# Two layers of a hybrid diffusion backbone on one core: the last two token tiles of the attention output projection, staggered by two weight rows

## The chip, the cores and the metric

The kernel is one program on one core of a Trainium2 chip. The metric is device time in microseconds (us) of one execution. The core has five engines, each with its own queue of instructions that it works off in order: TensorE (PE in the profile; PEld is its weight load), VectorE (DVE), ScalarE (ACT), GpSimd (POOL), and SyncE (SP), which here only issues DMAs. Engines wait for each other through semaphores. Matmul results land in PSUM, in banks of 128 x 512 floats; everything else lies in SBUF.

## The reference

Two layers over 1024 latent tokens (8 tiles of 128) and 256 context tokens. Layer 0 mixes tokens by a chunked gMLP, layer 1 by windowed attention; each is followed by a convolutional GLU. The change lies where layer 1's attention ends and its GLU begins:

```
y = moveaxis(out, 0, 1).reshape(bsz, n_tok, N_HEADS * HEAD_DIM) @ w_o      # output projection
x = x + g1 * rms_norm(y, norm_g[i, 1])
h = modulate(rms_norm(x, norm_g[i, 2]), sh2, sc2)
# conv_ffn(h):
a, b = split(h @ w_up, 2)              # 2 x 2816 columns
a = conv3(a) + conv_b                  # along the tokens
x = x + g2 * rms_norm((gelu(a) * b) @ w_down, norm_g[i, 3])
```

All of it is float32. The kernel multiplies by splitting each operand into a high part (`fp32r`) and a rest, so that one product is three matmuls: high x high, high x rest, rest x high.

## The kernel before, in words

`last_o` is the output projection of the last two token tiles, 6 and 7. The weight `w_o` comes in eight rows of 128 x 1024 (row k = 0 to 7): a DMA into `raw` (3 buffers), a cast on ScalarE into `wh`, and a subtraction on VectorE into `wl` (4 buffers each, shared with all other weights). Then twelve matmuls of 512 columns: for tile 6 and then tile 7, for both halves of 512 output columns, three each. The accumulators are two PSUM tiles `psA` of two banks; each holds one half of the columns for *both* token tiles, tile 6 in the first bank and tile 7 in the second.

After the eighth row each tile goes through `late_norm`, a generator with one step per `yield`: (1) load the residual row, sums of squares of both halves on ScalarE, products with the gate on VectorE; (2) the power on GpSimd, the residual sum on VectorE; (3) a second sum of squares on ScalarE, a power and the scaling of the row on GpSimd; (4) the flip: eight transposes on TensorE into a `psA` tile, scaled out of it by ScalarE and VectorE in turn, and a DMA of the flipped tile to `xT` in memory. `post_norm` is the like chain for tiles 4 and 5, which are in work when `last_o` starts (`tick` moves them on).

`lat_ffn` is the GLU. It needs its operands in eight combinations (`cmb`) of the flipped tiles: `combine(0)` builds them for tokens 0 to 511, `combine(1)` for 512 to 1023, in 16 steps each, from `xT`. `last_o` and the flips are the generator `between`: each of the 16 steps of `combine(0)` moves `between` one step. Then come the jobs. The first five column blocks of `w_up` are `up_plain` jobs, which need only the first half of the tokens: an X half of 48 matmuls of about 256 columns into two `psB` banks, and a Y half of 48 into a `psA` tile; weights again by cast and subtraction. After each quarter of a job, `step(fill)` moves the rest of `between` and then `combine(1)` one step. The jobs that follow need both halves of the operands.

The scheduler of the tile framework then lays out each engine's queue by its own estimates; in it, the X halves of jobs 1 and 2 come right after `last_o`, and the flips of tiles 6 and 7 stand inside job 2's X half.

Of the kernel before, what the change touches and what calls it, by code (L numbers as in the profile page):

```python
# [15 lines left out]
P = 128  # L16
D = 1024
KD = D // P
# [14 lines left out]
def hybrid_kernel(  # L33
# [23 lines left out]
    V, S, G, T = Engine(nc.vector, "V"), Engine(nc.scalar, "S"), Engine(nc.gpsimd, "G"), Engine(nc.tensor, "T")  # L57
    Q = Engine(nc.sync, "Q")
# [17 lines left out]
    def nm(s):  # L76
        uid[0] += 1
        return f"{s}_{uid[0]}"

    def t_raw():  # L80
        return sb.tile([P, 1024], F32, name=nm("raw"), tag="raw", bufs=3)

    def t_row(dt=F32, shape=(P, 1024)):
        return sb.tile(list(shape), dt, name=nm("row"), tag="row", bufs=10)
# [19 lines left out]
    def t_sm(w=2):  # L104
        return sb.tile([P, w], F32, name=nm("sm"), tag="sm", bufs=24)

    def t_w(tag, dt=F32R, shape=(P, 1024)):
        return sb.tile(list(shape), dt, name=nm(tag), tag=tag, bufs=4)
# [21 lines left out]
    def mm3(p, wh, wl, xh, xl, first, last):  # L130
        T.matmul(p, wh, xh, start=first, stop=False)
        T.matmul(p, wh, xl, start=False, stop=False)
        T.matmul(p, wl, xh, start=False, stop=last)
# [111 lines left out]
    gates = {}  # L245
# [5 lines left out]
    def step(gen, n=1):  # L251
        for _ in range(n):
            next(gen, None)
# [10 lines left out]
    def src_row(stage, t):  # L264
        if stage == 0:
            return x_in[0, t * P:(t + 1) * P, :] if t < 8 else ctx_in[0, (t - 8) * P:(t - 7) * P, :]
        return xs[stage][t * P:(t + 1) * P, :]
# [16 lines left out]
    def normed(src, dst, spare=None):  # L284
        r = rstd_of(src, spare)
        G.tensor_scalar(out=dst, in0=src, scalar1=r, scalar2=0.0, op0=ALU.mult, op1=ALU.add)
# [79 lines left out]
    active, mode = [], {"wide": False}  # L366

    def tick():
        for gen in list(active):
            if next(gen, 1):  # L370
                active.remove(gen)
# [8 lines left out]
    def gated(p, gate, y, part, junk):  # L380
        ss = t_sm(1)
        S.activation(junk, p, AF.Square, accum_out=ss)
        V.tensor_tensor(out=y, in0=p, in1=gate, op=ALU.mult)
        G.tensor_scalar(out=ss, in0=ss, scalar1=1.0 / D, scalar2=part, op0=ALU.mult, op1=ALU.add)
        return ss

    def late_norm(stage, t, banks, gate, mod, on_flip):
        xr = t_row()
        Q.dma_start(xr, src_row(stage, t))
        y = t_row()  # L390
        ss = EPS
        for h in range(2):
            hs = slice(h * 512, (h + 1) * 512)
            ss = gated(banks[h], gate[:, hs], y[:, hs], ss, y.bitcast(mybir.dt.bfloat16)[:, 1024 * h:1024 * h + 512])
        yield 0
        r = t_sm(1)
        G.tensor_tensor(out=r, in0=ss, in1=mhalf, op=ALU.pow)
        V.scalar_tensor_tensor(out=xr, in0=y, scalar=r, in1=xr, op0=ALU.mult, op1=ALU.add)
        yield 0
        normed(xr, y, y)  # L400
        S.dma_start(xs[stage + 1][t * P:(t + 1) * P, :], xr)
        yield 0
        xt = flip(stage + 1, t, y, mode["wide"], mod)
        on_flip(t, xt)

# [570 lines left out]
    def lat_ffn(l, stage, n0, halos, gate, between, steady, ctx=None, after=None):  # L976
# [120 lines left out]
        def up_plain(f, nxt, fill):  # L1097
            W, more = next_weights(nxt)
            X, X2, pY = psB(), psB(), psA()
            Y, Y2 = pY[:, 0, :], pY[:, 1, :]  # L1100
            for pair_, half in ((("b11", "b21"), X), (("b12", "b22"), Y)):
                for q in range(2):
                    for k in range(4):
                        wh, wl = (W[pair_[q]][z][:, k, :] for z in range(2))
                        c, kk = k // 2, k % 2
                        first = HL["a11" if q == 0 else "a12", c]
                        second = [A21[c][:, z] for z in range(2)] if q == 0 else [t[:, :, 0:256] for t in HL["a22", c]]
                        lead = 2 if half is X else 0
                        for out, src, lo, n in ((half[:, 0:256 + lead], first, 2 - lead, 256 + lead),
                                                ((X2 if half is X else Y2)[:, 0:256], second, 0, 256)):  # L1110
                            st, sp = q == 0 and k == 0, q == 1 and k == 3
                            xh, xl = (t[:, kk, lo:lo + n] for t in src)
                            T.matmul(out, wh, xh, start=st, stop=False, skip_group_check=True)
                            T.matmul(out, wh, xl, start=False, stop=False, skip_group_check=True)
                            T.matmul(out, wl, xh, start=False, stop=sp, skip_group_check=True)
                    step(fill)
                    step(more)
                if half is X:
                    a = t_row(shape=(P, 1028))
                    G.memset(a[:, 0:1], 0.0)  # L1120
                    S.copy(a[:, 1:257], X[:, 2:258])
                    S.copy(a[:, 513:514], X[:, 1:2])
                    S.copy(a[:, 257:513], X2[:, 0:256])
                    G.tensor_copy(keep[:, f:f + 1], a[:, 512:513])
            step(more, 9)
            conv_gate(f, a, 512, pY[:, :, 0:256], 0)
# [70 lines left out]
        if ctx is not None:  # L1197
            fill = chain(between, combine(0), combine(1))
        else:
# [6 lines left out]
            fill = chain(between, combine(1))  # L1206
        for (f, how), nxt in zip(jobs, jobs[1:] + [None]):
# [3 lines left out]
            if fill is not None:  # L1211
                step(fill, 100)
                fill = None
# [30 lines left out]
        for h in range(2):  # L1244
            pair = [psA() for _ in range(2)]
            banks = [pair[i // 2][:, i % 2, :] for i in range(4)] + [psB() for _ in range(4)]
            ws = {}
# [30 lines left out]
            for i in range(8):  # L1278
# [14 lines left out]
                for q in range(2):  # L1293
                    hs = slice(q * 512, (q + 1) * 512)
# [391 lines left out]
    orow, last_rows = {}, {}  # L1686
# [89 lines left out]
    for i in range(n_pairs + LC):  # L1776
# [13 lines left out]
        if i in (21, 24, 27):  # L1790
            t = 5 + (i - 21) // 3
# [16 lines left out]
    def last_o():  # L1808
        tiles = sorted(last_rows)
        acc = [psA() for _ in range(2)]  # L1810
        for k in range(KD):
            raw = t_raw()
            Q.dma_start(raw, w_o[0, k * P:(k + 1) * P, :])
            hi, lo = t_w("wh"), t_w("wl")
            S.copy(hi, raw)
            V.tensor_sub(lo, raw, hi)
            for i, t in enumerate(tiles):
                oh, ol_ = last_rows[t]
                for h in range(2):
                    hs = slice(h * 512, (h + 1) * 512)  # L1820
                    mm3(acc[h][:, i, :], oh[:, k, :], ol_[:, k, :], hi[:, hs], lo[:, hs], k == 0, k == KD - 1)
            tick()
            yield
        for i, t in enumerate(tiles):
            active.append(late_norm(2, t, [acc[h][:, i, :] for h in range(2)], gates[(1, 2, 0)], (1, 3), on4))
            yield

    tick()
# [44 lines left out]
```

## Time and profile before

| | |
|---|---|
| runs of before, median (lowest to highest of 3) | 2944.5 us (2943.89 to 2946.25) |
| the profiled execution | 2941.13 us |
| its span, first to last instruction | 2939.4 us |
| mean granted TensorE clock | 0.991 |
| TensorE busy | 2830.1 us, 96% of the span |
| VectorE / ScalarE / GpSimd busy | 69% / 46% / 23% |
| idle time of TensorE from 2190 to 2275 us, longest wait | 9.6 us, for GpSimd (`row`) |

The span leaves out 1.73 us before the first and after the last instruction. A row of the timeline gives the start, the duration and what an instruction writes and reads; a bracket at its end gives the idle time of that engine just before and what ended it. Durations of matmuls in a row overlap, so the pace is read from starts, or from the busy time of a window and its count. PEclk is the share of full TensorE clock that was granted: 1.00 is the level of 2.4 GHz, 0.50 that of 1.2 GHz.

### The profile page before, as it was taken

To read this page: it belongs to the slowest core of one execution; us is meant where nothing else is said; L and a number is where in the kernel's file an instruction comes from. 1 tells how busy PE (TensorE), PEld (TensorE's weight loads), DVE (VectorE), ACT (ScalarE), POOL (GpSimd) and SP (SyncE) were. 2 spreads that over 40 slices of the span, in tenths; PEclk is the share of its full clock that TensorE was granted. 3 is DMA by queue.
4 is the path that set the end of the run, shared out by engine and by line. 5 is a ranking of instruction groups with operands and counts; after the bars stand their busy time and mean duration, and the time that the engine had idled before them with its cause. 6 is when DMAs were issued, how large, how long until landed. Compare 5 with 4: busy or idle time off the path is not lost. (4 is left out here: it accounts for less than half of the span.)

```text
span 2939.4 us, 40162 instructions
## 1 busy us (share of the span) xinstructions
PE 2830.1 (96%) x14834; PEld 2406.6 (82%) x14834; DVE 2033.0 (69%) x3066; ACT 1353.9 (46%) x2279; POOL 683.9 (23%) x1003
## 2 busy tenths in 40 slices
PE   7999999999999999999999999899998999999999
PEld 5798988899898888888777777888887888888887
DVE  6557674756787878778643769887877777776333
ACT  4332342322575444543323534877775444444221
POOL 1151130720201212220003025564551212220000
PEclk9999999999999999999999999999999999999999
DMA  7764356532675333546845865356666333325532
GB/s 260 239 190 143 111 183 211 163 98 75 195 232 164 108 115 101 172 144 233 292 133 186 274 227 170 107 192 215 195 230 195 108 112 104 97 83 189 181 114 100
DMA packets 402310, 488.08 MB, mean 166 GB/s; under 512 B 17473, under 2 KB 296897, under 8 KB 402113
## 3 DMA queue, kind: packets, MB, share of 16 engines
q1 hardware_dynamic: 345697, 422.32, 44.8%
q10 hardware_dynamic: 55264, 58.99, 5.9%
q0 software_dynamic: 1152, 4.19, 0.4%
q8 instruction: 117, 1.92, 0.3%
q14 instruction: 80, 0.66, 0.1%
HBM read 388.96 MB, written 96.47 MB: 165 GB/s over the span
## 5 line engine op out<-in xcount | busy, mean ns | idle before, releaser
L50 PE MATMUL psB<-cmb,wh 128*128 128x512 f32 (+2 forms) x2584 | 757.3, 377 | 5.7 <-ACT row L50 2.6
L50 ACT CAST wh<-raw 128x1024 fp32r<-128x1024 f32 (+1 forms) x388 | 346.2, 904 | 490.8 <-PE psB L50 207.0
L50 PEld LDWEIGHTS psB<-cmb,wh 128*128 128x128 f32 x2584 | 472.2, 189 | 104.0 <-ACT row L50 4.9
L50 PE MATMUL psB<-cmb,wl 128*128 128x512 f32 (+2 forms) x1292 | 487.4, 377 | 0.0
L50 DVE TENSOR_TENSOR wl<-raw,wh 128x1024 fp32r<-128x1024 f32 (+1 forms) x388 | 400.0, 1043 | 124.2 <-ACT wh L50 119.7
L50 PE MATMUL psB<-wh,big 128*128 128x512 f32 x864 | 288.3, 401 | 1.4 <-ACT big L50 1.3
L50 PEld LDWEIGHTS psB<-cmb,wl 128*128 128x128 f32 x1292 | 243.6, 189 | 48.2
L50 POOL TENSOR_SCALAR sm<-sm 128x1 f32<-128x1 f32 (+1 forms) x76 | 41.3, 544 | 870.6 <-ACT tmp L50 320.6
L50 POOL TENSOR_TENSOR row<-raw,raw 128x512 f32<-128x512 f32 x44 | 76.4, 1736 | 602.1 <-DMA raw<-in_f_w_up_dram 485.9
L50 DVE TENSOR_TENSOR al<-raw,ah 128x1024 fp32r<-128x1024 f32 x74 | 90.5, 1224 | 170.9 <-ACT ah L50 170.5
L50 PE MATMUL psB<-wh,act 128*128 128x512 f32 x640 | 202.9, 395 | 1.6 <-DVE tmp L50 1.6
L50 PEld LDWEIGHTS psB<-wh,big 128*128 128x128 f32 x864 | 163.4, 190 | 41.1 <-ACT big L50 2.4
L50 PE MATMUL psA<-big,wh 128*128 128x320 f32 x1024 | 193.3, 311 | 3.0 <-ACT wh L50 1.8
L50 DVE SCALAR_TENSOR_TENSOR row<-row,cwcols,row 128x1024 f32<-128x1024 f32 (+2 forms) x142 | 160.9, 1133 | 38.4 <-issue 17.8
L50 ACT CAST ah<-raw 128x1024 fp32r<-128x1024 f32 x74 | 77.4, 1048 | 226.8 <-PE psB L50 158.8
L50 ACT CAST wh<-row 128x512 fp32r<-128x512 f32 (+1 forms) x132 | 100.7, 765 | 167.8 <-DVE row L50 77.4
L50 PE MATMUL psB<-wl,big 128*128 128x512 f32 x432 | 167.8, 398 | 0.0
L50 PEld LDWEIGHTS psA<-big,wh 128*128 128x128 f32 x1024 | 159.7, 188 | 4.0 <-ACT wh L50 2.3
L50 POOL TENSOR_SCALAR row<-row,sm,sm 128x128 f32<-128x128 f32 x160 | 122.1, 778 | 148.0 <-DMA row<-vscr 147.3
L50 PEld LDWEIGHTS psB<-wh,act 128*128 128x128 f32 x640 | 120.1, 188 | 30.1 <-issue 1.0
L50 PE MATMUL psB<-row,wh 128*128 128x256 f32 x744 | 138.9, 288 | 4.2 <-ACT row L50 1.5
L50 PE MATMUL psA<-wh,ah 128*128 128x512 f32 x336 | 133.6, 398 | 7.1 <-DVE y L50 7.1
(264 smaller groups left out, 6235.0 us busy)
## 6 DMA issues: line engine op xcount, KB each, us to landing
raw<-in_f_w_up_dram SPq DMA_DIRECT2D x142, 512.0 KB, 4.3
raw<-actd SPq DMA_DIRECT2D x83, 512.0 KB, 4.5
raw<-in_a_w_in_dram SPq DMA_DIRECT2D x64, 512.0 KB, 4.7
raw<-in_ada_w_dram SPq DMA_DIRECT2D x64, 512.0 KB, 4.7
wh<-woscr SPq DMA_DIRECT2D x48, 512.0 KB, 4.4
raw<-in_f_w_down_dram SPq DMA_DIRECT2D x88, 256.0 KB, 3.7
actd<-row SPq DMA_DIRECT2D x39, 512.0 KB, 2.6
raw<-in_a_w_out_dram SPq DMA_DIRECT2D x35, 512.0 KB, 3.4
```

What stands on the lines that cost most here:

```text
L50: ins = fn(*a, **kw)
```

## The change

Tile 7 now follows two weight rows behind tile 6: the loop of `last_o` has ten steps, tile 6 takes rows 0 to 7 in steps 0 to 7, tile 7 in steps 2 to 9. The flips of tiles 6 and 7 get two more steps before them (`rest=2`; the other caller of `late_norm` keeps 0). And `up_plain` moves `fill` twice after each quarter of a Y half, so six steps for a job and not four. Products, sums and weights are the same ones.

```
-    def late_norm(stage, t, banks, gate, mod, on_flip):
+    def late_norm(stage, t, banks, gate, mod, on_flip, rest=0):
...
-        yield 0
+        for _ in range(1 + rest):
+            yield 0
         xt = flip(stage + 1, t, y, mode["wide"], mod)
...
-                    step(fill)
+                    step(fill, 2 if half is Y else 1)
...
-        for k in range(KD):
-            raw = t_raw()
...
-            for i, t in enumerate(tiles):
-                oh, ol_ = last_rows[t]
-                for h in range(2):
-                    hs = slice(h * 512, (h + 1) * 512)
-                    mm3(acc[h][:, i, :], oh[:, k, :], ol_[:, k, :], hi[:, hs], lo[:, hs], k == 0, k == KD - 1)
-            tick()
+        ws = {}
+
+        def tile_mm(i, k):
+            if not 0 <= k < KD:
+                return
+            oh, ol_ = last_rows[tiles[i]]
+            for h in range(2):
+                hs = slice(h * 512, (h + 1) * 512)
+                mm3(acc[h][:, i, :], oh[:, k, :], ol_[:, k, :], ws[k][0][:, hs], ws[k][1][:, hs], k == 0, k == KD - 1)
+
+        for k in range(KD + 2):
+            if k < KD:
+                raw = t_raw()
+                Q.dma_start(raw, w_o[0, k * P:(k + 1) * P, :])
+                ws[k] = t_w("wh"), t_w("wl")
+                S.copy(ws[k][0], raw)
+                V.tensor_sub(ws[k][1], raw, ws[k][0])
+            tile_mm(0, k)
+            tile_mm(1, k - 2)
+            if k < KD:
+                tick()
             yield
         for i, t in enumerate(tiles):
-            active.append(late_norm(2, t, [acc[h][:, i, :] for h in range(2)], gates[(1, 2, 0)], (1, 3), on4))
+            active.append(late_norm(2, t, [acc[h][:, i, :] for h in range(2)], gates[(1, 2, 0)], (1, 3), on4, 2))
```

The scheduler moves rows in the queues with it. First TensorE, at the flips of tiles 4 and 5 (`psB<-ident`), early in `last_o`; `row_20110` and `row_20111` are tile 6's operands, `row_20573` and `row_20574` tile 7's. Before:

```order
L50 MATMUL psA_20635<-wl_20661,row_20573 128x512
L50 MATMUL psA_20635<-wh_20660,row_20574 128x512
L50 MATMUL psB_20677<-ident,acc_19583 128x128 x4
L50 MATMUL psB_20678<-ident,acc_19583 128x128 x4
L50 MATMUL psB_20697<-ident,acc_19584 128x128 x4
L50 MATMUL psB_20698<-ident,acc_19584 128x128 x4
L50 MATMUL psA_20634<-wh_20722,row_20110 128x512
```

and now, where `wh_20710` is row 2's weight:

```order
L50 MATMUL psA_20634<-wh_20710,row_20110 128x512
L50 MATMUL psA_20635<-wh_20710,row_20110 128x512
L50 MATMUL psB_20665<-ident,acc_19583 128x128 x4
L50 MATMUL psB_20666<-ident,acc_19583 128x128 x4
L50 MATMUL psA_20634<-wl_20711,row_20110 128x512
L50 MATMUL psA_20634<-wh_20710,row_20111 128x512
L50 MATMUL psB_20685<-ident,acc_19584 128x128 x4
L50 MATMUL psB_20686<-ident,acc_19584 128x128 x4
L50 MATMUL psA_20635<-wl_20711,row_20110 128x512
L50 MATMUL psA_20635<-wh_20710,row_20111 128x512
L50 MATMUL psA_20634<-wh_20638,row_20573 128x512
```

Before, 24 of the 96 matmuls of `last_o` stand ahead of these flips (rows 0 and 1 of both tiles); now 14 do (rows 0 and 1 of tile 6 and two matmuls of row 2), two stand between the flips, and tile 7 starts behind them.

Second VectorE, in the same stretch, around the subtraction for weight row 4. Before (`wl_20765` is row 4's):

```order
L50 TENSOR_TENSOR wl_20723<-raw_20720,wh_20722 128x1024
L50 TENSOR_TENSOR wl_20744<-raw_20741,wh_20743 128x1024
L50 TENSOR_SCALAR row_20676<-psB_20677,modc 128x128
L50 CAST cmb_20599<-row_20676 128x2x2
L50 TENSOR_TENSOR wl_20765<-raw_20762,wh_20764 128x1024
L50 TENSOR_TENSOR cmb_20600<-row_20630,cmb_20599 128x2x256
```

and now (`wl_20753` is row 4's, `wl_20774` row 5's):

```order
L50 TENSOR_TENSOR cmb_20608<-row_20648,cmb_20607 128x2x256
L50 TENSOR_TENSOR row_20648<-row_20648,row_20630 128x512
L50 TENSOR_TENSOR row_20649<-row_20630 128x512
L50 TENSOR_TENSOR row_20649<-row_20631,row_20648 128x512
L50 TENSOR_TENSOR wl_20753<-raw_20750,wh_20752 128x1024
L50 TENSOR_TENSOR cmb_20604<-row_20648,cmb_20603 128x2x256
L50 TENSOR_TENSOR wl_20774<-raw_20771,wh_20773 128x1024
L50 TENSOR_TENSOR cmb_20612<-row_20649,cmb_20611 128x2x256
```

Row 4's subtraction was the third instruction after row 3's; now 25 stand between them: the eight that scale the flips of tiles 4 and 5 out of PSUM, eight small ones for the edge of the convolution, and nine of `combine(0)`.

Third SyncE, the loads at the end of `last_o` (`row<-xs` is the residual row of tile 6 and then of tile 7). Before:

```order
L50 DMA raw_20954<-in_f_w_up_dram 128x8x128
L50 DMA row_20854<-xs_93 128x1024
L50 DMA raw_20955<-in_f_w_up_dram 128x8x128
L50 DMA raw_20997<-in_f_w_up_dram 128x8x128
L50 DMA row_20865<-xs_93 128x1024
L50 DMA raw_20998<-in_f_w_up_dram 128x8x128
```

and now:

```order
L50 DMA raw_20916<-in_f_w_up_dram 128x8x128
L50 DMA row_20860<-xs_93 128x1024
L50 DMA raw_20917<-in_f_w_up_dram 128x8x128
L50 DMA raw_20955<-in_f_w_up_dram 128x8x128
L50 DMA raw_20956<-in_f_w_up_dram 128x8x128
L50 DMA raw_21133<-in_f_w_up_dram 128x8x128
L50 DMA row_20871<-xs_93 128x1024
```

Tile 7's residual row moved behind two more weight loads, the second of them job 3's.

Further on, the flip of tile 6 stands behind 65 matmuls of jobs 1 and 2 and no longer behind 52, that of tile 7 fourteen matmuls behind it and no longer ten, and 23 matmuls of job 3's X half now come ahead of job 1's Y half. VectorE's list from the first scaling of tile 4's flip to the last instruction before the first scaling of tile 6's flip is the same but for a few: it gains two subtractions for `cmb`, and one weight subtraction moves behind it.

## Rows read from the trace of the kernel before

**Rows 1.** The page, part 1: busy us of each engine.

```profile
PE 2830.1 (96%) x14834; PEld 2406.6 (82%) x14834; DVE 2033.0 (69%) x3066; ACT 1353.9 (46%) x2279; POOL 683.9 (23%) x1003
```

**Rows 2.** Timeline of TensorE, 2190 to 2275: start, us, what, [idle before <- releaser].

```profile
2192.77 0.39 PE L50 MATMUL psA<-wh,row 128*128 128x512 f32 x1
...
2196.09 0.50 PE L50 MATMUL psA<-wh,row 128*128 128x512 f32 x1 [2.93 <-ACT row L50]
...
2198.59 1.65 PE L50 MATMUL psA<-wh,row 128*128 128x512 f32 x3 [1.32 <-DVE row L50]
...
2203.23 1.03 PE L50 MATMUL psB<-ident,acc 128*128 128x128 f32 x8
2205.04 1.09 PE L50 MATMUL psB<-ident,acc 128*128 128x128 f32 x8 [0.77 <-POOL acc L50]
...
2216.09 0.50 PE L50 MATMUL psA<-wl,row 128*128 128x512 f32 x1 [1.18 <-DVE wl L50]
...
2224.06 0.40 PE L50 MATMUL psB<-cmb,wh 128*128 128x258 f32 x2
...
2240.03 1.97 PE L50 MATMUL psA<-ident,row 128*128 128x128 f32 x8 [9.64 <-POOL row L50]
...
2250.44 0.50 PE L50 MATMUL psA<-cmb,wh 128*128 128x256 f32 x2 [0.51 <-DVE row L50]
...
2270.03 0.80 PE L50 MATMUL psB<-cmb,wh 128*128 128x258 f32 x2 [2.25 <-ACT row L50]
```

**Rows 3.** Windows: stretch, its us; busy us (count) by engine; PEclk, DMA share, GB/s.

```profile
2198.00:2200.70 2.70, 2.11 (x5) 1.72 (x6) 2.70 (x3) 1.03 (x3) 2.39 (x3) 0.51 0.21 86
...
2204.36:2238.07 33.71, 24.17 (x132) 20.41 (x132) 32.12 (x53) 23.57 (x42) 7.40 (x8) 0.96 0.80 245
2206.10:2224.06 17.96, 16.78 (x73) 13.24 (x72) 17.58 (x35) 12.67 (x24) 0.00 (x0) 1.00 0.85 249
2224.06:2240.03 15.97, 6.33 (x53) 6.11 (x52) 13.12 (x16) 9.16 (x18) 8.49 (x9) 0.86 0.79 248
2240.03:2245.90 5.87, 5.87 (x28) 5.87 (x29) 0.41 (x1) 0.47 (x2) 1.85 (x3) 0.51 0.35 93
...
2269.90:2272.60 2.70, 2.57 (x12) 2.58 (x13) 2.70 (x5) 2.70 (x7) 1.07 (x2) 0.50 0.03 6
```

**Rows 4.** Timeline of GpSimd.

```profile
2200.18 2.67 POOL L50 TENSOR_SCALAR acc<-row,rstT 128x1024 f32<-128x1024 f32 x1
...
2233.71 4.42 POOL L50 TENSOR_SCALAR sm<-sm 128x1 f32<-128x1 f32 x1 [4.28 <-ACT row L50]
...
2238.86 1.12 POOL L50 TENSOR_SCALAR row<-row,rstT 128x1024 f32<-128x1024 f32 x1
```

**Rows 5.** Groups of VectorE's instructions, 2204.3 to 2238.1: busy us, mean ns.

```profile
L50 DVE TENSOR_TENSOR wl<-raw,wh 128x1024 fp32r<-128x1024 f32 x9 | 10.8, 1222 | 1.0 <-ACT wh L50 1.0
L50 DVE TENSOR_TENSOR cmb<-row,cmb 128x512 fp32r<-128x512 f32 x12 | 8.1, 688 | 0.3 <-ACT cmb L50 0.3
L50 DVE TENSOR_TENSOR row<-row,row 128x512 f32<-128x512 f32 x6 | 4.1, 690 | 0.0
L50 DVE TENSOR_SCALAR row<-psB,modc 128x128 f32<-128x128 f32 x8 | 2.8, 406 | 2.4 <-ACT row L50 2.4
...
L50 DVE SCALAR_TENSOR_TENSOR row<-row,sm,row 128x1024 f32<-128x1024 f32 x2 | 2.5, 1280 | 0.0
...
L50 DVE CAST cmb<-row 128x4 fp32r<-128x4 f32 x4 | 0.6, 182 | 0.0
```

**Rows 6.** Timeline of ScalarE, and of its DMA queue (ACTq).

```profile
2223.56 0.60 ACT L50 ACTIVATE row<-psA 128x512 bf16<-128x512 f32 x1 [1.45 <-PE psA L50]
...
2232.47 1.05 ACT L50 ACTIVATE row<-row 128x1024 bf16<-128x1024 f32 x1
...
2252.56 0.52 ACTq L50 DMA_DIRECT2D xT<-row  x1
```

**Rows 7.** DMA issues, 2180 to 2262: tile, queue, count, KB each, us to landing.

```profile
row<-xs SPq DMA_DIRECT2D x2, 512.0 KB, 5.5
```

More of the change, by code (lines that the diff above doesn't have):

```diff
@@ L1810, in last_o @@
         acc = [psA() for _ in range(2)]
-        for k in range(KD):
-            raw = t_raw()
[L1813 to L1816, printed above, removed]
-            for i, t in enumerate(tiles):
-                oh, ol_ = last_rows[t]
-                for h in range(2):
-                    hs = slice(h * 512, (h + 1) * 512)
-                    mm3(acc[h][:, i, :], oh[:, k, :], ol_[:, k, :], hi[:, hs], lo[:, hs], k == 0, k == KD - 1)
-            tick()
+        ws = {}
[17 more added lines that the diff above has]
+                tick()
             yield
         for i, t in enumerate(tiles):
-            active.append(late_norm(2, t, [acc[h][:, i, :] for h in range(2)], gates[(1, 2, 0)], (1, 3), on4))
+            active.append(late_norm(2, t, [acc[h][:, i, :] for h in range(2)], gates[(1, 2, 0)], (1, 3), on4, 2))
             yield
```

## The prediction, written before the changed kernel was run

> **What bounds the kernel now.** I read the page's busy shares first: TensorE works 96% of the span [rows 1], so a change can win only what TensorE idles, or loses at the lower clock, where it acts. Then the timeline of TensorE around `last_o` with its brackets [rows 2]: the idle pieces from 2193 to 2271 are 2.93, 1.32, 0.77, 1.18, 9.64, 0.51 and 2.25 us, 18.6 in all. The windows [rows 3] give the clock: after the first piece it is granted 0.51 (the 1.2 GHz level) from 2198.0 to 2200.7, after the long one 0.51 from 2240.03 to 2245.90, after the last 0.50 for 2.7 us, each time loaded. Work done at half clock is lost by half: 1.3, 2.9 and 1.3 us, so 24 us is all that lies here, 0.8% of the span.
>
> The long piece is the wait for tile 6's flip: the last matmul of `last_o` is followed by 52 matmuls of jobs 1 and 2, then the transposes wait from 2230.4 to 2240.03 for GpSimd's scaled row. Who is late? GpSimd's one-column operation on the sum of squares took 4.42 us, from 2233.71 to 2238.13 [rows 4], and ended when VectorE's run did: VectorE was busy 32.12 of the 33.71 us from 2204.36 to 2238.07 [rows 3]. In that stretch VectorE is the engine at its limit, and the flip comes 2 us behind the end of its list.
>
> **The change, part by part.**
>
> *Tile 6 done earlier.* On TensorE tile 6 ends 18 matmuls before tile 7. That brings nothing by itself: both tiles share the two PSUM tiles, and before, ScalarE's first square of tile 6 waited until 2223.56 [rows 6], when tile 7's last matmul into the first of them was just over, although tile 6's own last one there stands six matmuls further up. I take the same wait for the changed kernel.
>
> *The flips of tiles 4 and 5.* Their row is ready at 2202.85 (GpSimd's 2.67 us from 2200.18 [rows 4]), and all that makes it stands unchanged in its queues. Only 14 matmuls of `last_o` are now ahead of it. The six of row 0 end at 2193.16 as before; eight more at 0.23 us (16.78 us for 73 [rows 3]) end at about 2195.0. So TensorE idles 7.9 us there, in place of 2.93 + 1.32. By the clock seen after 9.64 us of idling, the next 5.9 us run at 0.5 and lose up to 2.9 us (1.3 before). At the end of the second flip, 2206.1 before, 80 of the 96 matmuls are left, not 72: 8 x 0.23 = 1.9 us to do later.
>
> *Weights two rows longer.* A weight buffer is free only after tile 7's use, and row 4's subtraction stands behind 25 instructions on VectorE. By the groups [rows 5]: 8 x 0.41 + 8 x 0.18 + 4 x 0.69 + 5 x 0.69 + its own 1.22 = 12.2 us from 2204.4, so row 4 is whole at about 2216.5 (at 2213.5 if the small ones and half of the scalings cost nothing, beside ScalarE's work; at 2218 if the second flip comes 1.5 us late at half clock). TensorE has 20 matmuls until then, 4.6 us from 2206.1, or 6.3 at half clock: it reaches row 4 at 2210.7 to 2212.4 and idles some 4 to 5 us. Row 6 likewise: nine VectorE instructions, 5 x 0.69 + 2 x 0.69 + 2 x 1.22 = 7.3 us, make it whole at 2223.8; TensorE comes there with 24 matmuls, 2222.1, and idles 1.7 us. From there 10 matmuls (2.3 us) bring it to row 7, whole 2 x 0.69 + 1.22 = 2.6 us after row 6, 2226.4; with 24 more `last_o` ends at about 2231.9, against 2224.06. That is 7.8 us later. VectorE never has less to do for it: its list is the old one, plus two of 0.69 and less one of 1.22.
>
> *From the end of `last_o` (E) to the flip of tile 6.* Before it took 15.97 us. Now less of the list is left. The last cast of a weight before the squares needs tile 7's row 6 done, so its subtraction ends at E + 0.9; then, in VectorE's order, product, product, `row`, product, product (0.6 from start to start) to E + 3.9, tile 6's residual sum (1.28) to E + 5.1, ScalarE's square (1.05 and its read-out [rows 6]) to E + 6.4. GpSimd's small operation then meets tile 7's residual sum and four more subtractions on VectorE, 0.69 x 3 + 1.22 = 3.3 us, and I let it wait as in [rows 4], to E + 9.3; its power and scaling took 1.9 us (2238.13 to 2240.03). The flip is at E + 11.2 = 2243.1, three us later than before. TensorE fills 65 x 0.12 = 7.8 us of that (6.33 us for 53 [rows 3]), and idles 3.4 in place of 9.64.
>
> *From that flip to job 4.* The next place where TensorE waited is 2270.03, for ScalarE's copy out of `psB`, whose queue stood behind the operands of `combine(1)`: flip of tile 6 to the DMA of tile 7's flip 12.5 us (2240.03 to 2252.56 [rows 6]), from there to job 4 17.5 us. The second stays: the queues read alike. The first had 2.9 us lost to the clock and now has four more matmuls between the flips: 10 us at full clock, 12.5 at half, I take 11. Job 4 starts at 2243.1 + 11 + 17.5 = 2271.6, 1.6 us later than before. TensorE will have waited some 5 us for it, not 2.25, so the 1.3 us at half clock after it grow to about 2.
>
> *Six steps of `fill` in a job.* `combine(1)` is two steps later at its start and done within three jobs, not four. From job 4 to the first full job TensorE had no wait to win or lose: it was bound by its own work. I cost this at nothing; its cover is TensorE's work in the jobs before the first full one. If ScalarE's heavier queue kept a copy back beyond it, the price would be a wait like the 2.25 us.
>
> Sum: 1.6 + 0.7 = 2.3 us slower. On the profiled execution, 2941.13, that is 2943.4; the median of the runs shown stands 3.4 us above it, so **2946.8 us**. My error in the two ends (row 4 at 2213.5 to 2218, flip to DMA 10 to 12.5 us) makes this case's own range 2942 to 2951.
>
> A rule speaks for less. In the Trainium skill, "SBUF — State Buffer", section "SBUF: two separate sides", a VectorE operation with two SBUF inputs and a GpSimd operation share a port pair, and whichever starts first holds it for that whole instruction. The 4.42 us agree that GpSimd waits; but by the rule's letter it need not wait for a gap in VectorE's list, only for the end of one instruction.
>
> **The rivals.**
>
> *GpSimd gets in early* (this is what the rule would give). If the small operation waits one subtraction and not four, the flip is at E + 8.4, and job 4 starts 2.8 us earlier: 2946.8 - 2.8 = 2944.0. For it: the 2.67 us of a scaling beside two subtractions, against 1.12 alone [rows 4], is a delay of little more than one of them. Against it: the 4.42 us were spent at this very place, with three weight subtractions behind each other.
>
> *The stagger works, the weights keep up.* If rows 4 to 7 are ready in time (instructions overlap, ScalarE casts early), only the 7.9 us remain of the idling and only its 2.9 us of the clock: 2944.5 - 18.6 - 5.5 + 7.9 + 2.9 = 2931 at best, and 2937 with half of the way. For it: the same 96 matmuls and the same list on VectorE, and the idle piece of 9.64 us stands where the change acts. Against it: the 25 instructions before row 4, and 95% of VectorE in use.
>
> *Slower: tile 7's residual row comes late.* Its load now stands behind job 3's weight load, which needs a `raw` buffer that VectorE frees only about 1.5 us before E. By the 5.5 us that these loads took [rows 7] it lands at E + 4 to 5, just before VectorE comes to tile 7's residual sum. If it lands later than E + 5.1, VectorE's queue stands, and with it the weights of jobs 2 and 3 and all evictions; the price is the delay, 3 to 6 us, and the same for the loads of the second half of `combine(0)`, which now come before row 7's: 2946.8 + 6 = 2953.
>
> **How the numbers follow.** The forecast has 0.52, GpSimd early 0.10, the stagger that works 0.19, the late row 0.19. Two runs of this kernel are told apart from about 0.2%, 5.9 us: faster than 2938.6 are most of the stagger that works and a lower edge of the forecast, 0.19; slower than 2950.4 are most of the late row and an upper edge of the forecast, 0.20; the rest, 0.61, is no change. The range that leaves 2 in 10 out takes the forecast, GpSimd early and half of either side: 2937 to 2952.
>
> **What would show it.** In the timeline of TensorE: the transposes of tile 4 after an idle piece of 7 to 8 us that ends near 2202.9; a wait of 3 us or more for `wl` at row 4 and a smaller one at row 6; the end of `last_o` at 2229 to 2234; the wait before tile 6's flip at 2 to 5 us; job 4 at 2268 to 2276. In the windows, clock 0.5 after the flips of tiles 4 and 5. On ScalarE, tile 6's squares not before tile 7's last matmuls. I am wrong if the weights of rows 4 to 7 show no wait, if the flip of tile 6 does not come behind VectorE's list, or if the jobs after 2300 show new waits.

## The result and the profile after

The changed kernel took 2951.84 us in the median of 11 runs (2947.16 to 2958.27). The kernel before, run beside it, took 2946.25. The ratio is 1.0019 [1.0011, 1.0026]: 5.6 us slower, on the edge of what can be told from no change. The forecast was 2.3 us slower and 2946.8 us. The time lies 0.2 us inside the range of 2937 to 2952, and outside the 2942 to 2951 that the forecast gave for its own case. Of the 5.0 us above the forecast 1.75 are the kernel before, whose median was 2944.5 in the three runs that the forecast started from.

The busy shares of the changed kernel read as in [rows 1]; TensorE's busy time over the whole span is within 1 us of before:

```profile
PE 2830.9 (96%) x14834; PEld 2406.1 (82%) x14834; DVE 2030.0 (69%) x3066; ACT 1353.8 (46%) x2279; POOL 673.7 (23%) x1003
```

Where the time went is seen in the stretch from the first matmul of `last_o` to the first matmul of the first full job (512 columns). It holds the same work in every kernel of this study (613 or 614 matmul records). The windows of that stretch, of before and then of the changed kernel (window, its length, then busy time and count of PE, PEld, DVE, ACT and POOL, granted clock, DMA share, GB/s):

```profile
2191.25:2299.97 108.72, 90.12 (x614) 83.66 (x612) 81.19 (x122) 62.73 (x115) 29.38 (x34) 0.92 0.59 183
```

```profile
2192.13:2305.93 113.80, 92.08 (x614) 85.08 (x612) 80.41 (x122) 63.35 (x116) 22.20 (x34) 0.90 0.58 181
```

It is 5.1 us longer: length less busy time gives 21.7 us of idling against 18.6, and 2.0 us more of the same matmuls for the lower clock. Ahead of the stretch the two executions differ by 0.9 us, behind it by less than 0.1. Below, places are given from the first matmul of the stretch (2191.25 before, 2192.13 now), so that the 0.9 us doesn't count.

TensorE's timeline in the changed kernel, the rows with a wait in brackets and the flips (start, length, engine, instruction, the idle time ahead and what ended it); they answer to [rows 2]:

```profile
2203.86 1.97 PE L50 MATMUL psB<-ident,acc 128*128 128x128 f32 x8 [7.64 <-POOL acc L50]
2206.48 1.86 PE L50 MATMUL psB<-ident,acc 128*128 128x128 f32 x8
2214.36 0.73 PE L50 MATMUL psA<-wh,row 128*128 128x512 f32 x2 [1.39 <-ACT wh L50]
2217.47 0.50 PE L50 MATMUL psA<-wl,row 128*128 128x512 f32 x1 [2.37 <-DVE wl L50]
2244.32 1.10 PE L50 MATMUL psA<-ident,row 128*128 128x128 f32 x8 [3.89 <-POOL row L50]
2247.90 1.64 PE L50 MATMUL psA<-ident,row 128*128 128x128 f32 x8
2252.33 0.51 PE L50 MATMUL psB<-cmb,wh 128*128 128x258 f32 x2 [0.79 <-ACT wh L50]
2253.59 0.38 PE L50 MATMUL psB<-cmb,wl 128*128 128x258 f32 x1 [0.51 <-DVE wl L50]
2275.48 0.80 PE L50 MATMUL psB<-cmb,wh 128*128 128x258 f32 x2 [5.06 <-ACT row L50]
```

The wait of 9.64 us became 3.89. Against that stand 7.64 ahead of tile 4's flip (2.93, 1.32 and 0.77 around it before), 3.76 at weight row 4 and 5.06 ahead of job 4 (2.25 before). The clock in four windows of the changed kernel (same columns as above) was at the 1.2 GHz level behind three of these pieces:

```profile
2203.86:2206.48 2.62, 2.62 (x11) 2.32 (x12) 0.54 (x2) 0.91 (x2) 1.85 (x3) 0.50 0.92 316
2244.32:2245.42 1.10, 1.10 (x10) 1.10 (x11) 0.00 (x0) 0.00 (x0) 0.87 (x3) 1.00 1.07 318
2245.42:2249.30 3.88, 3.88 (x23) 3.88 (x22) 0.41 (x1) 0.46 (x1) 1.01 (x2) 0.56 0.11 34
2275.48:2278.00 2.52, 2.52 (x11) 2.52 (x12) 2.52 (x5) 2.52 (x6) 1.08 (x2) 0.50 0.53 185
```

Last, how tile 6 gets from its flip to job 4. First the two writes of the flipped tiles on ScalarE's queue in before (the first of them and, from [rows 6], the second 2.14 us later), with the loads that wait for them on SyncE's queue:

```profile
2250.42 0.52 ACTq L50 DMA_DIRECT2D xT<-row  x1
...
2258.36 0.88 SPq L50 DMA_DIRECT2D row<-xT  x2
```

Then the same in the changed kernel, with the square of tile 6 ahead and the copy that released job 4 behind (the group of two writes begins at 2255.66, the second at 2256.57):

```profile
2232.63 0.58 ACT L50 ACTIVATE row<-psA 128x512 bf16<-128x512 f32 x1
...
2255.66 1.45 ACTq L50 DMA_DIRECT2D xT<-row  x2
2256.57 0.54 ACTq L50 DMA_DIRECT2D xT<-row  x1
...
2267.96 0.62 ACT L50 CAST cmb<-row 128x512 fp32r<-128x512 f32 x1 [5.22 <-DMA row<-xT]
2275.01 0.69 ACT L50 COPY row<-psB 128x256 f32<-128x256 f32 x3
...
2263.97 0.88 SPq L50 DMA_DIRECT2D row<-xT  x2
```

Tile 6's write was issued 59.2 us into the stretch before and 63.5 us now; the loads followed 7.9 and 8.3 us behind it, and job 4 19.6 and 19.8 us behind it. So of the 4.6 us by which job 4 comes later, 3.4 are the later flip, 1.0 the longer way from the flip to the write (11.3 us, not 10.4) and 0.2 what follows. What lies between the flip and the write stands in the queues of ScalarE and VectorE. ScalarE's, before (`row_20903` is tile 6's flip, `row_20922` tile 7's):

```
ACTIVATE row_20922<-psA_20923,modc 128x128
ACTIVATE row_20903<-psA_20904,modc 128x128
CAST wh_21168<-raw_21134 128x1024
DMA xT_98<-row_20903 1024x1x128
ACTIVATE row_20922<-psA_20923,modc 128x128
DMA xT_98<-row_20922 1024x1x128
```

and now (`row_20987` is tile 6's, `row_21006` tile 7's):

```
CAST wh_21137<-raw_21133 128x1024
ACTIVATE row_20987<-psA_20988,modc 128x128
ACTIVATE row_21006<-psA_21007,modc 128x128
CAST wh_21168<-raw_21134 128x1024
ACTIVATE row_20987<-psA_20988,modc 128x128
ACTIVATE row_21006<-psA_21007,modc 128x128
DMA xT_98<-row_20987 1024x1x128
DMA xT_98<-row_21006 1024x1x128
```

In both, the evictions of the two tiles take turns, and each tile's pieces take turns between ScalarE and VectorE. Now two weight casts stand among them, and tile 6's write stands behind tile 7's last piece. The order costs time in two ways that the trace of the changed kernel shows on ScalarE and VectorE:

```profile
2249.57 0.46 ACT L50 ACTIVATE row<-psA,modc 128x128 f32<-128x128 f32 x1 [3.66 <-PE psA L50]
...
2254.09 1.22 DVE L50 TENSOR_TENSOR wl<-raw,wh 128x1024 fp32r<-128x1024 f32 x1
2255.22 0.72 DVE L50 TENSOR_SCALAR row<-psA,modc 128x128 f32<-128x128 f32 x2
```

ScalarE's second piece is tile 7's, and it waits until tile 7's flip is done, with tile 6's next piece behind it (3.66 us; 3.40 before). And each weight cast brings a subtraction of 1.2 us on VectorE with the next pieces behind that. The write at 2255.66 followed tile 6's last piece, which is VectorE's (2255.22, 0.41 us), at once.

### The profile page after: what moved, and what is told of

The parts are those of the page before. It is cut to its first block, busy times and chain, and to the rows that moved or that the text cites. A ratio compares the mean times of both kernels' runs of the same rounds, so it can differ in the third digit from the quotient of the medians.

```text
span 2945.4 us, 40169 instructions
## 1 busy us (share of the span) xinstructions
PE 2830.9 (96%) x14834; PEld 2406.1 (82%) x14834; DVE 2030.0 (69%) x3066; ACT 1353.8 (46%) x2279; POOL 673.7 (23%) x1003
## 5 line engine op out<-in xcount | busy, mean ns | idle before, releaser
L50 PEld LDWEIGHTS psB<-cmb,wl 128*128 128x128 f32 x1292 | 243.4, 188 | 48.9 <-DVE wl L50 0.7
```

Of the source, the lines that this page charges most:

```text
L50: ins = fn(*a, **kw)
```

## The experiments

All ratios are to the kernel before, five rounds each. The stretch is the one above; idle is its length less TensorE's busy time. Flip 6 is the start of tile 6's flip from the first matmul, "to write" the time from there to the first of the two writes. All from one profiled execution each.

| kernel | ratio | stretch us | busy | idle | flip 6 | to write |
|---|---|---|---|---|---|---|
| before | | 108.7 | 90.1 | 18.6 | 48.8 | 10.4 |
| control | 0.9998 [0.9989, 1.0007] | 110.6 | 93.2 | 17.4 | 51.0 | 10.4 |
| changed | 1.0019 [1.0011, 1.0026] | 113.8 | 92.1 | 21.7 | 52.2 | 11.3 |
| stag_only | 1.0015 [1.0005, 1.0025] | 111.7 | 94.0 | 17.6 | 52.0 | 10.8 |
| no_stag | 1.0009 [1.0000, 1.0018] | 113.4 | 92.8 | 20.6 | 50.4 | 12.1 |
| rest_only | 1.0006 [0.9998, 1.0015] | 111.3 | 91.5 | 19.8 | 49.9 | 12.2 |
| fill_only | 0.9991 [0.9980, 1.0003] | 109.1 | 90.3 | 18.8 | 48.9 | 10.4 |
| acc_before | 1.0014 [1.0005, 1.0022] | 114.4 | 94.8 | 19.6 | 50.0 | 12.4 |
| acc_after | 1.0017 [1.0007, 1.0028] | 113.4 | 93.8 | 19.6 | 51.4 | 11.1 |
| rest_split | 1.0011 [1.0003, 1.0020] | 111.4 | 91.8 | 19.6 | 51.5 | 11.9 |
| eng_after | 0.9994 [0.9984, 1.0004] | 106.3 | 89.5 | 16.8 | 52.0 | 4.3 |
| eng_before | 0.9979 [0.9969, 0.9990] | 106.4 | 91.1 | 15.3 | 51.1 | 4.9 |
| eng_fill | 0.9986 [0.9974, 0.9998] | 105.3 | 89.9 | 15.4 | 51.2 | 4.9 |
| eng_stag1 | 0.9973 [0.9961, 0.9986] | 102.3 | 89.3 | 13.0 | 50.5 | 4.1 |

The stretch of a kernel against the mean of before and control (109.7 us) goes with its ratio: +4.1 us is 1.0014 of the span (changed, 1.0019 measured), +4.7 is 1.0016 (acc_before, 1.0014), -3.3 is 0.9989 (eng_before, 0.9979), -7.4 is 0.9975 (eng_stag1, 0.9973). None of the 13 is off by more than 0.0010. But the sign goes with the stagger: of the six kernels that have one, five lie 0.0004 to 0.0008 above what their stretch gives, and of the seven without, five lie 0.0002 to 0.0010 below. So the stretch may not hold all that the stagger costs; what the rest is, these runs don't show.

**The kernel before once more** (control, no edit).

> The kernel before once more, unchanged. It shows how far two executions of one kernel differ at these places, since stag_only, no_stag, acc_before and acc_after all came out 0.09 to 0.17% slower and each profiled execution starts the projection at another time (2191 to 2203 us). Theory (the places are set by the order in the queues): from the first matmul of the projection to the first full job 108.7 us within 1 us, the first of the two xT writes about 2 us ahead of the second, time 0.9993 to 1.0007. Rival (the profiled execution of before was a favourable draw): 111 to 114 us from the same place, as in the other kernels, so that the trace's 5 us are no cost of the change.

The time is the same, and the queues gave the same waits, but the stretch was 1.9 us longer: the projection ran longer at the lower clock and ended 35.2 us in, not 32.6, and tile 6's flip moved by 2.2. Neither reading was quite right; a difference of 2 us in one trace is within what one kernel does.

**The stagger alone** (stag_only: the new loop of `last_o`, `late_norm` with its old rest, one fill).

> The stagger of two weight rows alone; flips without the two steps of rest, one fill per Y quarter as before. Theory (the loss is the stagger's: flips of tiles 4 and 5 come 14 matmuls into the projection, weight row 4 comes late, last_o ends later and the chain behind it starts later): the wait before the flip of tile 4 is 7 to 8 us, a wait of 2 to 5 us for wl at row 4, last_o ends some 6 to 8 us later than before, job 4 starts 3 to 5 us later than before; time 1.0010 to 1.0020 of before. Rival (the operand build in more places, or the later flips, cost the time): the same two waits are seen but are given back, job 4 starts where it did, and the time is 0.9995 to 1.0005.

The waits of 7.64 and 2.37 us are there and `last_o` ends 41.2 us in. But TensorE's idle time is no longer than in before; what it has more is busy time at the lower clock, and job 4 doesn't wait; 3.77 us of waiting stand at a Y part instead, on TensorE, with the two writes on ScalarE's queue:

```profile
2266.18 0.80 PE L50 MATMUL psA<-cmb,wh 128*128 128x256 f32 x2 [3.77 <-DVE row L50]
...
2266.16 1.25 ACTq L50 DMA_DIRECT2D xT<-row  x2
```

The Y part needs one of the two `psA` tiles, and the flips hold both. So the last piece of tile 6's evictions releases two things at once: its write and this matmul. The same wait is 2.65 us in no_stag and in rest_only and 4.55 in acc_before, each time ended within 0.1 us of the first write. The kernel is slower, as the theory had it, but without the late job 4 that was to make it so.

**The other two parts without the stagger** (no_stag: `rest` 2 and two fills, old loop).

> The other two parts without the stagger: flips of tiles 6 and 7 two steps later, two fills per Y quarter. Theory (the loss is the stagger's): flip of tile 4 waits about 3 us as before, last_o ends within 1 us of before, job 4 within 1 us, time 0.9993 to 1.0005. Rival (these two parts cost it): job 4 is 2 to 5 us later with last_o unmoved, time 1.0010 to 1.0020. A third reading: two loads of xT rows issued together land 1.2 us later, as in the changed kernel (6.8 against 5.6 us), whenever fill runs twice; then job 4 is 1 to 2.5 us later and the time 1.0003 to 1.0009.

The theory that the loss is the stagger's alone falls here, by the trace: flip of tile 4 and end of `last_o` stand as before (32.9 us), and yet the stretch is 2.8 us longer than in control and 4.7 longer than in before. ScalarE's queue has both writes at the end of the evictions, as in the changed kernel, 12.1 us behind the flip. The time, 1.0009 [1.0000, 1.0018], doesn't decide: it is in the third reading's range, and its interval reaches into the other two.

**The later flips alone** (rest_only) **and the fills alone** (fill_only).

```
-            active.append(late_norm(2, t, ..., (1, 3), on4))
+            active.append(late_norm(2, t, ..., (1, 3), on4, 2))
```

> The later flips alone (two more steps before the flips of tiles 6 and 7), no stagger, one fill. TensorE's order is that of before, ScalarE's differs: the evictions of the two flips alternate to the end and both xT writes are issued one behind the other, and one more cast of a weight stands behind them. Theory (the two writes together land later, and job 4 waits for the second): second write as far from the flip as in before, 12 to 13 us, landing 5.9 to 6.8 us instead of 5.6, first full job 2 to 5 us later than in before, time 1.0004 to 1.0015. Rival (only the stagger costs): within 1 us, time 0.9995 to 1.0005.

```
-                    step(fill)
+                    step(fill, 2 if half is Y else 1)
```

> Two fills per Y quarter alone. All queues are as before up to the second job's Y part, and the two writes stand as before. Theory (this part costs nothing): the same place to the first full job within 1 us of before, time 0.9995 to 1.0005. Rival (ScalarE's heavier queue keeps a copy back, the price named in the prediction): job 4 or one of its neighbours waits 2 us or more longer, time 1.0007 to 1.0015.

The fills cost nothing. The later flips change only the order of evictions and writes; the first write is 1.8 us later, the stretch 0.6 to 2.5 us longer than in the two executions of before. The ratio can't be told from 1.

**PSUM tiles cut by token tile** (acc_before, acc_after).

```
-   mm3(acc[h][:, i, :], ...)      late_norm(2, t, [acc[h][:, i, :] for h in range(2)], ...)
+   mm3(acc[i][:, h, :], ...)      late_norm(2, t, [acc[i][:, h, :] for h in range(2)], ...)
```

> The kernel before with the two PSUM tiles of the projection cut by token tile and not by column half. Theory (tile 6's squares wait for tile 7's matmuls because the PSUM tile is shared, but VectorE's list sets the flip): tile 6's squares start up to 1.4 us (six matmuls) earlier, the flip of tile 6 moves by 0 to 1.5 us, time 0.9993 to 1.0003. Rival (PSUM sharing is what makes the 9.64 us wait): the wait before that flip falls by 3 us or more, time 0.9988 or less.

> The changed kernel with the PSUM tiles cut by token tile. Theory 1 (the shared PSUM tile takes the stagger's use away): tile 6's first square starts 3 to 4 us before tile 7's last matmul of the projection instead of beside it, tile 6's flip comes 2 to 4 us earlier than in the changed kernel, its wait of 3.9 us goes; the wait of 7 to 8 us at tile 4's flip and that for row 4's weights stay, so 2 to 4 us below the changed kernel: 1.0005 to 1.0012 of before. Theory 2 (VectorE's list sets the flip, the PSUM tile nothing): the squares start earlier but the flip of tile 6 stays within 1 us of the changed kernel's, time 1.0015 to 1.0022.

In acc_after tile 6's first square and tile 6's flip read, on ScalarE, GpSimd and TensorE:

```profile
2235.85 0.59 ACT L50 ACTIVATE row<-psA 128x512 bf16<-128x512 f32 x1
...
2243.82 4.10 POOL L50 TENSOR_SCALAR sm<-sm 128x1 f32<-128x1 f32 x1 [1.06 <-ACT row L50]
...
2249.82 1.97 PE L50 MATMUL psA<-ident,row 128*128 128x128 f32 x8 [5.57 <-POOL row L50]
```

The square now starts 1.9 us ahead of tile 7's last matmul (2237.70), and the flip came 0.8 us earlier than in the changed kernel, not 2 to 4: theory 2. GpSimd's one-column operation took 4.10 us here; what was won at the square was lost beside VectorE's list. In acc_before the wait ahead of the flip fell from 9.64 to 5.60 us, but the flip itself stayed between those of before and control: `last_o` ended 3.7 us later than in before, with waits of 1.51 and 2.37 us at a weight row. Its time, 1.0014, is above both readings. Its first write is the latest of all, 12.4 us behind the flip.

**The two writes separated** (rest_split: the changed kernel with `rest` 1 for tile 6 and 3 for tile 7).

> The changed kernel with rests of one step for tile 6 and three for tile 7. Up to the flip of tile 6 all is as in the changed kernel; then 78 matmuls and not 14 stand between the flips, so tile 6's evictions and its xT write are done before tile 7's flip, and the two writes are separated. Theory (the second xT write sets job 4): tile 6's write goes 3 us or more earlier than in the changed kernel, tile 7's 3 to 6 us later and lands in 5.6 us or less, job 4 starts as much later, waits 7 to 10 us, time 1.0025 to 1.0040 of before. Rival (ScalarE's list of casts and fills sets job 4, the writes are hidden): job 4 within 1.5 us of the changed kernel, time 1.0014 to 1.0022.

Neither. Tile 6's write was not earlier (two weight casts stand among its pieces), tile 7's came 5 us later, and job 4 did not wait; 4.17 us of waiting stand at a Y part instead. The loads of both tiles followed 3.6 us behind the second write (2270.81 to 2274.44), against 7.4 us in the changed kernel and 5.8 in before, where the writes are 0.9 and 2.1 us apart. But the other write is not all that differs: a weight load of 512 KB was issued 0.33 us ahead of the second write in before and of the first in the changed kernel (here 2.2 us ahead of the second). On SyncE's queue, of before and then of the changed kernel:

```profile
2252.23 0.37 SPq L50 DMA_DIRECT2D raw<-in_f_w_up_dram  x1
```

```profile
2255.33 0.37 SPq L50 DMA_DIRECT2D raw<-in_f_w_up_dram  x1
```

In eng_fill below, with writes 2.2 us apart as in before and no weight load near them, the loads followed 4.0 us behind the second. So what writing together costs is not shown apart from the weight loads.

**One engine for each tile's evictions** (eng_before, eng_after, eng_fill). If the first write sets job 4, it must go earlier when tile 6's pieces don't wait for tile 7's:

```
-            if k % 2:
+            if (k % 2 if t not in (6, 7) or stage != 3 else t == 7):
                 V.tensor_scalar(out=xt[:, k, :], ...
```

> The changed kernel, but the eight evictions of tile 6's flip all on ScalarE and those of tile 7's all on VectorE, instead of ScalarE and VectorE by turns on both tiles. Theory (job 4 starts 19.2 to 19.8 us behind the issue of the first of the two xT writes, in before, its repetition, the changed kernel and acc_after; that write waits 10.4 to 11.3 us behind the flip for evictions that go by turns and for weight casts between them): the first write comes 4 to 6 us behind the flip, the operands of job 4 are there 4 us or more earlier, no wait of 5 us before job 4 or in its place, first full job 108 to 111.5 us from the projection's first matmul instead of 113.8, time 0.9995 to 1.0008 of before. Rival (the stagger's late end of the projection and VectorE's list cost the time; the writes are hidden): the wait turns up at the next Y part or job, first full job at 113 us or later, time 1.0013 to 1.0022.

> The kernel before with the same evictions (tile 6's on ScalarE, tile 7's on VectorE). Theory: first write 4 to 6 us behind the flip instead of 10.4, the wait of 2.25 us at job 4 and the half clock behind it go, first full job 105.5 to 108.5 us from the projection's first matmul (108.7 and 110.6 in the two profiled executions of before), time 0.9983 to 0.9998. Rival (that wait is set by ScalarE's copies): it stays, time 0.9996 to 1.0005.

> The same with two fills per Y quarter, the part of the change that cost nothing by itself (0.9991). Theory: as eng_before, 0.9980 to 0.9997; if the fills bring anything, it is the 1 to 2.5 us of the wait that fill_only showed at the Y part near 81.6 us, which goes with the earlier writes. Rival: no difference from fill_only, 0.9988 to 1.0003.

eng_before, on TensorE, ScalarE, VectorE and the two queues:

```profile
2246.05 1.97 PE L50 MATMUL psA<-ident,row 128*128 128x128 f32 x8 [9.21 <-POOL row L50]
2249.97 1.91 PE L50 MATMUL psA<-ident,row 128*128 128x128 f32 x8
...
2248.06 2.90 ACT L50 ACTIVATE row<-psA,modc 128x128 f32<-128x128 f32 x8 [6.42 <-PE psA L50]
2251.00 0.52 ACTq L50 DMA_DIRECT2D xT<-row  x1
2254.59 0.52 ACTq L50 DMA_DIRECT2D xT<-row  x1
...
2251.92 2.64 DVE L50 TENSOR_SCALAR row<-psA,modc 128x128 f32<-128x128 f32 x8 [7.82 <-PE psA L50]
...
2258.54 0.88 SPq L50 DMA_DIRECT2D row<-xT  x2
```

Eight pieces take 2.90 us on ScalarE, and the write goes 4.95 us behind the flip. From there to the end of the stretch the timeline of TensorE has no wait; the 9.21 us ahead of the flip stay. The same in the changed kernel (eng_after) leaves 0.58 of its 5.06 us:

```profile
2254.14 1.31 PE L50 MATMUL psA<-ident,row 128*128 128x128 f32 x8 [3.75 <-POOL row L50]
...
2278.97 0.51 PE L50 MATMUL psB<-cmb,wh 128*128 128x258 f32 x2 [0.58 <-ACT row L50]
```

The mechanism holds in all three; the sizes were off in two: eng_after's stretch of 106.3 us is under the 108 to 111.5 expected, and the times of eng_after and eng_before lie just under their ranges. The stretches of eng_after and eng_before are 0.1 us apart: with the writes early, the change neither costs nor gains in the stretch of these two traces.

The times say otherwise. Eng_after's median was 2948.12 us and eng_before's 2943.51, 4.6 us apart, against 5.6 for the change without this edit; and the edit gains about as much on the kernel before (to 0.9979) as on the changed one (from 1.0019 to 0.9994). So early evictions shorten both kernels, but that the late writes are what the change costs is seen only in the stretch of single traces. What eng_after loses outside the stretch, these runs don't show. Nor does the edit separate the write from the `psA` tile, which comes free as early.

**A stagger of one row on top** (eng_stag1: eng_after with `tile_mm(1, k - 1)` and nine steps).

> eng_after with tile 7 one weight row behind tile 6 and not two. 20 matmuls of the projection stand ahead of tile 4's flip (24 without a stagger, 14 with two rows). Theory (the idle time is only moved between the flips of tiles 4 and 5 and that of tile 6, since VectorE's list sets tile 6's flip at 50 to 52 us from the projection's first matmul whatever the stagger): tile 4's flip waits about 6.3 us, tile 6's 4 to 6 us, first full job 105 to 107.5 us from the first matmul as in eng_after (106.3) and eng_before (106.4), time 0.9980 to 0.9997. Rival (a stagger that is matched to the queue gains): tile 6's flip at 48 us or less and first full job at 104 or less, time 0.9975 or less.

```profile
2206.82 0.50 PE L50 MATMUL psA<-wh,row 128*128 128x512 f32 x1 [1.53 <-ACT row L50]
2209.33 1.85 PE L50 MATMUL psA<-wh,row 128*128 128x512 f32 x4 [1.31 <-DVE row L50]
2213.64 1.97 PE L50 MATMUL psB<-ident,acc 128*128 128x128 f32 x8 [2.46 <-POOL acc L50]
2224.70 0.73 PE L50 MATMUL psA<-wh,row 128*128 128x512 f32 x2 [2.69 <-ACT wh L50]
2227.80 0.80 PE L50 MATMUL psA<-wl,row 128*128 128x512 f32 x1 [2.37 <-DVE wl L50]
2252.52 1.09 PE L50 MATMUL psA<-ident,row 128*128 128x128 f32 x8 [2.69 <-POOL row L50]
```

The flip is where the theory put it (50.5 us), but tile 4's flip waited 2.46 us and tile 6's 2.69, where 6.3 and 4 to 6 were expected, and the stretch is 4 us shorter than in eng_before: 2.3 us less idling (15.3 to 13.0) and 1.9 us less for the clock. The idle time was not only moved: stretch and time are the rival's, though not its early flip. 0.9973 is the lowest ratio of the study; its interval overlaps with that of eng_before, so which of the two is faster stays open. Both intervals lie below 1.

## Why the prediction was right, and where it was not

| step | forecast | in the trace |
|---|---|---|
| wait ahead of tile 4's flip | 7.9 | 7.64 |
| wait for row 4's weight | 4 to 5 | 1.39 + 2.37 |
| wait for row 6's weight | 1.7 | none |
| end of `last_o`, against before | +7.8 | +7.6 |
| wait ahead of tile 6's flip | 3.4 | 3.89 |
| tile 6's flip | +3.1 | +3.4 |
| flip to the second write | 11 | 12.3 |
| second write to job 4 | 17.5 | 18.9 |
| job 4 | +1.6 | +4.6 |
| wait ahead of job 4 | some 5 | 5.06 |
| behind job 4 | +0.7 | +0.5 |
| sum | +2.3 | +5.1 |

**The mechanism was right up to the flip.** Waits, end of `last_o` and flip came within 1.7 us of their numbers. The end of `last_o` was luck in part: the 1.7 us of wait at row 6 did not come, but the clock fell to the 1.2 GHz level behind the wait at row 4, which the forecast did not have, and 3.2 us of matmuls ran at it, about 1.6 us lost:

```profile
2218.50:2221.70 3.20, 3.20 (x9) 2.46 (x8) 3.20 (x6) 2.03 (x4) 0.00 (x0) 0.50 1.03 361
```

And the "4 to 5 us" at row 4 is 4.1 to 5.8 by the prediction's own ends (2216.5 less 2210.7 to 2212.4). That shared PSUM tiles hold tile 6's squares back is seen in the trace (2232.63, with the last matmul of `last_o` at 2232.34), but acc_after shows that this is not what decides. That VectorE's list behind the squares does is read from the traces; no run made that list shorter.

**The step that failed** is "From that flip to job 4", in two sentences: "10 us at full clock, 12.5 at half, I take 11", and "The second stays: the queues read alike". I took the first as TensorE's time between flips and the second as fixed. But the evictions on ScalarE and VectorE, with the casts and subtractions between them, set the first, and a piece takes 0.46 and 0.41 us there at either level of TensorE's clock. In the second, the loads followed the write by 7.4 us and not 5.8, with the first write and two weight loads issued in the 3.1 us ahead of it, where before it was the first write and one. They were short by 1.3 and 1.4 us; with 0.3 us at the flip that is the 3 us by which job 4 was later than forecast, and so the sum was 2.3 us and not the 5.1 of the trace. Measured from the first write the chain is simpler: job 4 came 19.6, 19.2, 19.8 and 19.6 us behind it in the four kernels where it waited more than 1 us (before, control, changed, acc_after). Eng_after tested it as the lever: the write went 7 us earlier, and 0.58 of the 5.06 us were left.

**GpSimd early** was half right. The one-column operation took 0.57 us, not the 2.9 of wait that I added, but the scaling took 2.73 in place of 1.12 [rows 4], both beside VectorE's list:

```profile
2239.91 0.57 POOL L50 TENSOR_SCALAR sm<-sm 128x1 f32<-128x1 f32 x1 [2.19 <-ACT row L50]
2240.56 0.87 POOL L50 TENSOR_TENSOR rstT<-sm,mhalf 128x1 f32<-128x1 f32 x1
2241.54 2.73 POOL L50 TENSOR_SCALAR row<-row,rstT 128x1024 f32<-128x1024 f32 x1
```

```profile
2240.95 0.68 DVE L50 TENSOR_TENSOR row<-row,row 128x512 f32<-128x512 f32 x1
2241.55 1.22 DVE L50 TENSOR_TENSOR wl<-raw,wh 128x1024 fp32r<-128x1024 f32 x1
2242.68 0.68 DVE L50 TENSOR_TENSOR cmb<-row,cmb 128x512 fp32r<-128x512 f32 x1
```

Together the three are done 4.4 us behind the start of the first, against 4.8 forecast. The Trainium skill, "SBUF — State Buffer", section "SBUF: two separate sides", lets whichever operation starts first hold the port pair for its whole instruction. The 0.57 us agree; the same operation's 4.42, 4.57 and 4.10 us in before, control and acc_after, each longer than any one instruction of VectorE (1.28), do not.

**The stagger that works** fell by the weights of row 4, as argued against it. **The late residual row** came, and cost 0.56 us:

```profile
2239.14 1.28 DVE L50 SCALAR_TENSOR_TENSOR row<-row,sm,row 128x1024 f32<-128x1024 f32 x1 [0.56 <-DMA row<-xs]
```

**The six steps of fill** cost nothing, as forecast (fill_only 0.9991 [0.9980, 1.0003]).

## What to carry to other kernels

When a change moves the start of a chain, follow the chain through the queue of every engine that it crosses and look at the order of its last pieces, not only at the place where it starts: here the flip came 3.4 us late, and the pieces, casts and subtractions ahead of the store added 1.0. Two tiles that were both evicted by turns on two engines finished together and late here; one engine for each finished the first tile in half the time and spread the stores. Compare traces over a stretch that holds the same work in both, and profile the old kernel twice: two executions of it differed by 2 us in the stretch, and executions of the same code ahead of it by up to 12 us. And ask the times whether they agree: two kernels with equal stretches were 4.6 us apart.

## What the runs showed of the hardware that was not expected

- The same code ahead of the stretch took from 2191.08 us (control) to 2203.41 us (stag_only) in 14 profiled executions, more than any edit here moved. The five latest are kernels with a stagger (2198.40 to 2203.41); the sixth with one, the changed kernel, came at 2192.13. Whether that is chance, these runs don't show.
- Two stores of 512 KB on one queue, issued within 1 us of each other, kept the loads behind them 6.9 to 8.4 us from the issue of the first. The time went with the weight loads of 512 KB issued in the 2.6 us ahead: 8.3 to 8.4 us with two (changed, acc_before, acc_after), 6.9 to 7.1 with one (stag_only, no_stag, rest_only). In eng_fill, with none, it was 6.2 us, with the stores 2.2 us apart.
- In the changed kernel the granted clock fell once within a wait and once behind one. It was at 0.50 for the last 5.9 us of the wait ahead of tile 4's flip. But tile 6's flip ran at 1.00 for 1.1 us after 3.89 us of idling, and the next 3.9 us were granted 0.56. After 2.69 us of idling in eng_stag1, the 2.5 us that followed were granted 1.00. The first window is the changed kernel's, the second eng_stag1's:

```profile
2198.00:2203.86 5.86, 0.00 (x1) 0.01 (x1) 4.90 (x5) 2.13 (x4) 4.54 (x3) 0.50 0.65 236
```

```profile
2252.52:2255.00 2.48, 2.48 (x21) 2.48 (x22) 1.08 (x2) 1.35 (x4) 2.26 (x3) 1.00 0.72 211
```
